# Two changes to a two-layer decoder step: the small attention products of the first layer in two parts, and the second layer's gates without an absolute value

## The chip, the cores and the metric

The kernel runs on one core of one Trainium2 chip. The metric is the device time of one launch in microseconds (us), the median of three runs. The engines are named as in the profile: PE (TensorE, with PEld for its weight loads), DVE (VectorE), ACT (ScalarE), POOL (GpSimd) and SP, from whose queue all transfers of data start.

## What is computed

A step of a two-layer decoder with D = 1024 over 512 prompt tokens and 8 sequences of 8 sample tokens (576 tokens together). The first layer is a gated linear recurrence with 16 heads of 128. The second is sliding-window attention with 32 query heads over shared keys and values, whose output is multiplied by silu of a gate. Everything is in float32. The parts that the change touches:

```python
# first layer, per head and chunk of the recurrence
att = einsum('bhtsd,bhsd->bhts', qc[:, :, :, None, :] * exp(rel), kc)   # masked, causal
o = o + einsum('bhts,bhse->bhte', att, vc)
# second layer
q, gate = split(rms_norm(x, g_norm) @ w_in, 2, axis=-1)
return x + (o * silu(gate)) @ w_out
```

## The kernel before

**Products.** Float32 accuracy comes from splitting both operands of a large product into a high and a low part and adding three products: a 128 x 1024 block of weights arrives in a buffer raw, ACT casts it to whi (L200), and DVE (first layer) or POOL (second layer) subtracts to get wlo (L204). One projection of one head in the first layer is three terms of 16 matmuls of 288 columns (L228): xhi with whi, xlo with whi, xhi with wlo. The second layer makes the same in halves of the tokens (L211).

**First layer.** A head has four projections, in the order pf (forget gate, tile pf), pq (query), pi (value), pg (output gate), and a recurrence, head_rec. The two are two generators: woven runs the recurrence of head h while it advances the projections of head h + 1. At each `yield ASK[i]` the recurrence asks that so many twelfths of the projections be issued first: ASK begins 3, 4, 5, so one term of a product lies between two neighbouring yields. Every fourth head also has blocks of the output product (tile po) in that list, and the last head has those alone.

**The small products.** The chunk attention of a head is four chunks (NC) of 128 tokens, and each chunk is 20 small float32 products (L795) of 8 to 32 rows and 8 to 64 columns, placed in a 32-row part of the array by tile_position, all written to one PSUM tile pa. The trace counts 2,560 matmuls and 2,560 weight loads of L795 for the 16 heads, 160 of each per head. Two products smg (L806) for the sample tokens follow. Then DVE copies pa under a mask to att (L814) and smg to atts (L817). In the meantime DVE and ACT work on the forget gate of the next head: on DVE ka (L592) and lf (L595) read pf, ACT computes on them (L593, L596, L597), and DVE ends with L599. Later come pkt and pks (transposes), the states S (pu on PE, S on ACT at L848 and DVE at L850), and poT (L869, L887), which needs att and the states.

**Second layer.** Eight units (four groups of two); unit i has queries (q), gates (g) and an attention, and ORDER lists in which order the large products of q, g and o are issued while the attention steps run. An attention step makes the scores sc, DVE scales and reduces them (L1101, L1121), ACT takes exponentials (L1126), DVE and POOL scale (L1135), PE transposes (ptr, ptm), ACT and DVE split them (ph, pl at L1156, pk at L1163), PE makes pav, DVE joins it (ao, L1187) and multiplies by the gate (L1191, in place in sgt). A gate piece (m = 0 to 15, two per unit) is two half products pbg. ACT copies each to sgt (L1311), DVE copies the sample columns to sgS (L1313), and silu turns sgt into the gated factor: Abs, Exp, Ln on ACT (L1338 to L1340), min and subtract on DVE (L1341), Exp on ACT (L1342), and a multiply (L1343) on POOL, or on DVE for sgS.

**What sets the order.** A scheduler places each instruction on its engine's queue by priority; early(...) and high_priority move instructions forward. Each engine then runs its queue in order, and an instruction that waits for another engine holds all behind it.

The lines of silu before, where x is sgt or sgS and l a scratch tile:

```python
def silu(x, l, eng=dve):
    act.activation(l, x, AF.Abs)
    act.activation(l, l, AF.Exp, scale=-1.0)
    act.activation(l, l, AF.Ln, bias=1.0)
    dve.scalar_tensor_tensor(l, x, 0.0, l, ALU.min, ALU.subtract)
    act.activation(l, l, AF.Exp)
    eng.tensor_tensor(x, x, l, ALU.mult)
```

Of the kernel before, what the change touches and what calls it, by code (L numbers as in the profile page):

```python
# [15 lines left out]
AF = mybir.ActivationFunctionType  # L16
ALU = mybir.AluOpType
# [10 lines left out]
HN = T // 2  # L28
DI = 2048
NH = 16  # L30
NC = LP // P
# [6 lines left out]
SPAN = 40.0  # L38
# [13 lines left out]
ASK = (3, 4, 5, 6, 7, 8, 9, 10)  # L52
# [31 lines left out]
def yoco_kernel(  # L84
# [26 lines left out]
    act, dve, pool, pe, sp = nc.scalar, nc.vector, nc.gpsimd, nc.tensor, nc.sync  # L111
# [20 lines left out]
    def half(name):  # L132
        return ps["m"].tile([P, 512], F32, tag="m", name=name)

    def early(by=EARLY):
        return tc.high_priority(offset=by)
# [389 lines left out]
    with ExitStack() as actx:  # L526
# [153 lines left out]
        def head_rec(h, st, outs):  # L680
# [106 lines left out]
            part[16] = 0, 16, 16, 16  # L787
            turns = "64:0 64:1 32:2 0:3 0:2 24:3 0:1 32:0 8:3 24:2 16:3 0:0 8:2 24:1 16:2 8:1 24:0 16:1 8:0 16:0"
            for c in range(NC):
                for x in turns.split():  # L790
                    level, j = [int(v) for v in x.split(":")]
                    keys, queries = Ks[8 if level == 24 else level]
                    s0, ns, t0, nt = part[level]
                    s0, t0 = 32 * j + s0, (64 if level == 64 else 32 * j + t0)
                    pe.matmul(  # L795
                        pa[32 * j : 32 * j + ns, c, t0 : t0 + nt],
                        keys[:, c * P + s0 : c * P + s0 + ns],
                        queries[:, c * P + t0 : c * P + t0 + nt],
                        start=True,
                        stop=True,  # L800
                        tile_position=(0, 32 * j),
                    )
# [9 lines left out]
                    tile_position=(0, 32 * j),  # L812
                )
            dve.copy_predicated(att, view(m_ge, [[0, NC], [1, P]]), pa)  # L814
            yield ASK[1]
            ats = att_s[i2]
            dve.copy_predicated(  # L817
                view(ats[:LS, :], [[32, 4], [1, 16]]),
# [55 lines left out]
            for bb in [2 * j + i for i in range(2) for j in range(4)]:  # L874
                j = bb // 2
# [80 lines left out]
        for h in range(NH):  # L956
            nxt, chunks, n = {}, [], 0
# [21 lines left out]
    with ExitStack() as bctx:  # L979
# [34 lines left out]
        with tc.tile_pool(name="kvx", bufs=1) as kvx:  # L1014
# [4 lines left out]
            for c0 in range(0, 4, 2):  # L1019
                ws = [split_weights(kvw[c], f"kv{c}") for c in (c0, c0 + 1)]  # L1020
                kf = [kvx.tile([P, T], F32, tag=f"kf{c % 2}", name=f"kf{c}", bufs=2) for c in (c0, c0 + 1)]
                for j in range(2):
                    for c in range(2):
                        pm = half(f"pkv{c0 + c}_{j}")
# [274 lines left out]
        def gates(i, sgS, sgt):  # L1299

            g, pp = i // 2, i % 2
            for pr in range(2):
                m = 2 * i + pr
                c = DI + m * P
                w = split_weights(w_in_b[0, :, c : c + P].rearrange("(k p) c -> p k c", p=P), f"bg{m}")
                for j in range(2):
                    pm = half(f"pbg{m}_{j}")
                    product_half(pm, *w, bx, j)
                    n = min(HN, LP - j * HN)
                    with early(EARLYB):  # L1310
                        act.copy(sgt[:, pr, j * HN : j * HN + n], pm[:, :n])  # L1311
                        if j == 1:
                            dve.tensor_copy(sgS[:, 2 * pp + pr, :], pm[:, n:HN])  # L1313
                    if j == 1:
                        silu(sgt[:, pr, :], ab.tile([P, LP], F32, tag="lb", name=f"lb{m}", bufs=1), pool if SILU_POOL else dve)
                        if pp == 1 and pr == 1:
                            silu(sgS, ab.tile([P, 4, LS], F32, tag="oS", name=f"lbs{g}", bufs=1))
                    yield
# [16 lines left out]
                    yield  # L1335

        def silu(x, l, eng=dve):
            act.activation(l, x, AF.Abs)  # L1338
            act.activation(l, l, AF.Exp, scale=-1.0)
            act.activation(l, l, AF.Ln, bias=1.0)  # L1340
            dve.scalar_tensor_tensor(l, x, 0.0, l, ALU.min, ALU.subtract)  # L1341
            act.activation(l, l, AF.Exp)  # L1342
            eng.tensor_tensor(x, x, l, ALU.mult)  # L1343

        def new_group(g):
# [227 lines left out]
```

## Time and profile before

| what | value |
|---|---|
| median of three runs | 1188.15 us (1186.46 to 1188.95) |
| profiled execution | 1186.25 us, of which the span from first to last instruction is 1184.5 us |
| PE busy | 1115.6 us, 94% of the span, 10,937 matmuls |
| DVE busy | 901.2 us, 76% |
| ACT busy | 725.7 us, 61% |
| POOL busy | 340.2 us, 29% |
| mean granted PE clock | 0.977 of full speed |

Busy is the time in which an engine has an instruction in work. The idle time of PE is what is left of its span, 69 us. In a view of waits a line gives the engine that waits, the line waited for, and the sum; "issue" is time for which the profile shows no releaser. The first layer runs from about 30 us to 700 us in the profiled execution, the second from about 735 us to the end. The rows that are read are in the section ahead of the prediction.

### The profile page before, as it was taken

The page shows a single profiled execution, that of the slowest core. Times are in us where ns is not written, and L with a number is a line of the kernel's source. Part 1 is how long each engine was busy: PE and PEld are TensorE (multiplying, and loading weights), DVE is VectorE, ACT ScalarE, POOL GpSimd, SP SyncE. Part 2 cuts the span into 40 slices and gives each one's busy share as a digit, 9 for nine tenths or more (in the row PEclk, how much of TensorE's full clock was granted, in tenths as well). Part 3 has the DMA queues.
Part 4 walks back from the last instruction along what each step waited for, and adds up shares of the span by engine and source line. Part 5 has one row for each costly group of instructions (what it writes and reads, how often), then busy time and mean ns, then how long its engine had stood idle before and what let it go on. Part 6 is the DMA issues. An engine that isn't in the chain of part 4 may idle for free.

```text
span 1184.5 us, 27353 instructions
## 1 busy us (share of the span) xinstructions
PE 1115.6 (94%) x10937; PEld 1082.3 (91%) x10937; DVE 901.2 (76%) x2078; ACT 725.7 (61%) x1752; POOL 340.2 (29%) x311
## 2 busy tenths in 40 slices
PE   5999999998999989999999987989999989999997
PEld 4999999998998989999989877989989989998986
DVE  8897776589883597784887779567887788676686
ACT  6776763466772566762766455667746765776545
POOL 1122221121111132120212155544544453444440
PEclk8999999999999999999999998989999999999998
DMA  5332233232432423332332322211211212112102
GB/s 152 99 110 85 82 111 108 65 100 78 121 128 65 127 67 107 110 92 75 92 108 73 103 72 72 68 54 55 72 54 55 87 47 83 55 55 71 55 19 81
DMA packets 161097, 98.01 MB, mean 83 GB/s; under 512 B 3897, under 2 KB 157546, under 8 KB 160938
## 3 DMA queue, kind: packets, MB, share of 16 engines
q1 hardware_dynamic: 160970, 96.26, 27.7%
q8 instruction: 86, 1.41, 0.5%
q14 instruction: 41, 0.34, 0.1%
HBM read 84.06 MB, written 14.16 MB: 83 GB/s over the span
## 4 chain that ended last, share of the span: by engine, by line
PE 40%; DVE 13%; ACT 8%; issue 3%; POOL 1%; DVEq 0%; ACTq 0%; POOLq 0%
PE pbg L211 6%; PE po L211 5%; PE pbq L211 5%; PE po L228 4%; PE pg L228 3%; PE pf L228 3%; PE pi L228 2%; ACT P L1126 2%; PE pkv L211 2%; PE sc L1097 2%; PE pq L228 1%; DVE P L1101 1%; PE pav L1180 1%; PE pz L211 1%; DVE QS L1288 1%
## 5 line engine op out<-in xcount | busy, mean ns | idle before, releaser
L606 POOL TENSOR_TENSOR Xl<-Xl 128x72 f32<-128x72 f32 x80 | 50.1, 656 | 212.3 <-DVE Xl L603 211.1
L638 POOL TENSOR_TENSOR sg<-sg,lg 128x576 f32<-128x576 f32 x16 | 26.3, 1642 | 277.8 <-ACT lg L571 277.8
L200 ACT CAST whi_a<-raw_a 128x1024 fp32r<-128x1024 f32 x64 | 67.1, 1049 | 62.1 <-PE po L228 31.6
L204 DVE TENSOR_TENSOR wlo_a<-raw_a,whi_a 128x1024 fp32r<-128x1024 f32 x64 | 81.7, 1282 | 26.2 <-issue 24.2
L1126 ACT ACTIVATE P<-P,st 128x192 f32<-128x192 f32 (+2 forms) x128 | 54.2, 425 | 65.4 <-DVE st L1121 65.3
L1135 POOL TENSOR_SCALAR P<-P,st 128x192 f32<-128x192 f32 (+1 forms) x64 | 48.9, 774 | 110.6 <-DVE st L1128 87.1
L438 DVE TENSOR_TENSOR hT<-hT,po 128x576 f32<-128x576 f32 x32 | 24.1, 754 | 47.2 <-PE po L228 46.9
L200 ACT CAST whi_o<-raw_o 128x1024 fp32r<-128x1024 f32 x30 | 31.4, 1047 | 29.8 <-PE po L228 25.3
L204 POOL TENSOR_TENSOR wlo_bg<-raw_bg,whi_bg 128x1024 fp32r<-128x1024 f32 x16 | 38.3, 2396 | 32.7 <-ACT whi_bg L200 31.1
L228 PE MATMUL po<-oh,whi_o 128*128 128x288 f32 x256 | 43.4, 305 | 4.4 <-ACT whi_o L200 1.9
L211 PE MATMUL po<-ohb,whi_o 128*128 128x288 f32 x224 | 43.7, 311 | 2.3 <-DVE hT L1333 1.4
L211 PE MATMUL po<-olb,whi_o 128*128 128x288 f32 x224 | 42.2, 301 | 3.9 <-DVE olb L1395 2.0
L662 POOL TENSOR_TENSOR vb<-vst,bmask 128x512 fp32r<-128x512 f32 x32 | 36.7, 1167 | 26.7 <-DVE vst L658 13.8
L204 POOL TENSOR_TENSOR wlo_bq<-raw_bq,whi_bq 128x1024 fp32r<-128x1024 f32 x16 | 38.6, 2417 | 19.6 <-ACT whi_bq L200 19.5
L228 PEld LDWEIGHTS po<-oh,whi_o 128*128 128x128 f32 x256 | 36.9, 192 | 6.3 <-ACT whi_o L200 2.2
L228 PE MATMUL pq<-xhi,whi_a 128*128 128x288 f32 x256 | 38.4, 298 | 3.7 <-issue 3.7
L211 PE MATMUL pbq<-xhi,whi_bq 128*128 128x256 f32 (+1 forms) x256 | 41.7, 307 | 0.0
L211 PE MATMUL pbg<-xhi,whi_bg 128*128 128x288 f32 x256 | 41.3, 304 | 0.3 <-ACT QS L1285 0.3
L211 PE MATMUL pbq<-xlo,whi_bq 128*128 128x256 f32 (+1 forms) x256 | 41.1, 305 | 0.0
L228 PE MATMUL po<-ol,whi_o 128*128 128x288 f32 x256 | 41.0, 297 | 0.0
L211 PE MATMUL pbg<-xlo,whi_bg 128*128 128x288 f32 x256 | 40.9, 304 | 0.0
L211 PE MATMUL pbg<-xhi,wlo_bg 128*128 128x288 f32 x256 | 40.8, 303 | 0.0
(389 smaller groups left out, 3792.0 us busy)
## 6 DMA issues: line engine op xcount, KB each, us to landing
raw_a<-in_w_in_a_dram SPq DMA_DIRECT2D x64, 512.0 KB
S<-in_state_hgrn_dram SPq DMA_DIRECT2D x32, 256.0 KB
out_dram<-S SPq DMA_DIRECT2D x32, 256.0 KB
raw_o<-in_w_out_a_dram SPq DMA_DIRECT2D x16, 512.0 KB
raw_bq<-in_w_in_b_dram SPq DMA_DIRECT2D x16, 512.0 KB
raw_bg<-in_w_in_b_dram SPq DMA_DIRECT2D x16, 512.0 KB
raw_o<-in_w_out_b_dram SPq DMA_DIRECT2D x16, 512.0 KB
xt<-in_x_prompt_dram SPq DMA_DIRECT2D x4, 512.0 KB
```

The source lines that it names most:

```text
L200: act.copy(hi[:, :n], raw[:, :n])
L204: eng.tensor_tensor(lo[:, r], raw[:, r], hi[:, r].bitcast(F32), ALU.subtract)
L211: pe.matmul(pm[:, : c1 - c0], w[:, k * width + w0 : k * width + w0 + P], x(k)[i][:, c0:c1], start=n == 0, stop=n == len(terms) - 1,)
L228: pe.matmul(pm[:, j, :HN], w[:, k * width + c0 : k * width + c0 + P], x(k, j), start=n == 0 and k == 0, stop=n == 2 and k == nk - 1,)
L438: dve.tensor_add(h2, h2, ps2(pm))
L606: pool.tensor_tensor(X8[:, :, j : j + 1], X8[:, :, j : j + 1], X8[:, :, k : k + 1], ALU.add)
L638: (pool if SGP else dve).tensor_tensor(sg, sg, l, ALU.mult)
L662: pool.tensor_tensor(t, view(vst.bitcast(F32), [[0, 4], [1, P]], off=half * P), view(bmask, [[1, 4], [0, P]]), ALU.mult,)
L1097: pe.matmul(sc[:, hf, k0[hf] :], QS[pr][:, 2 * n + hf, :], kk[:, g, ks], start=q == 0, stop=q == 1)
L1101: dve.tensor_tensor_reduce(Pt[:, pr, hf, k0[hf] :], sc[:, hf, k0[hf] :], amask[:, k0[hf] :], 0.125, NEG, ALU.add, ALU.max, accum_out=st[:, ...
L1126: act.activation(x, x, AF.Exp, bias=st[:, a : a + 1], accum_out=st[:, 8 + a : 9 + a])
L1135: (pool if e == "p" else dve).tensor_scalar(x, x, st[:, 8 + a : 9 + a], None, ALU.mult)
```

## The change

The loop over the four chunks yields once in its middle, and the yield that stood between the two masked copies is gone. So the recurrence asks for the next step of the projections after two chunks instead of after four and smg. In the second layer DVE takes the halves of pbg out of PSUM, clamped from below at -40 (SPAN), and silu is x times exp(-ln(1 + exp(-x))): three activations instead of four, without the step on DVE. This is the form of the first layer's silu_arg.

```diff
--- before.py
+++ after.py
@@ -787,6 +787,8 @@
             part[16] = 0, 16, 16, 16
             turns = "64:0 64:1 32:2 0:3 0:2 24:3 0:1 32:0 8:3 24:2 16:3 0:0 8:2 24:1 16:2 8:1 24:0 16:1 8:0 16:0"
             for c in range(NC):
+                if c == NC // 2:
+                    yield ASK[1]
                 for x in turns.split():
                     level, j = [int(v) for v in x.split(":")]
                     keys, queries = Ks[8 if level == 24 else level]
@@ -812,7 +814,6 @@
                     tile_position=(0, 32 * j),
                 )
             dve.copy_predicated(att, view(m_ge, [[0, NC], [1, P]]), pa)
-            yield ASK[1]
             ats = att_s[i2]
             dve.copy_predicated(
                 view(ats[:LS, :], [[32, 4], [1, 16]]),
@@ -1308,9 +1309,9 @@
                     product_half(pm, *w, bx, j)
                     n = min(HN, LP - j * HN)
                     with early(EARLYB):
-                        act.copy(sgt[:, pr, j * HN : j * HN + n], pm[:, :n])
+                        dve.tensor_scalar(sgt[:, pr, j * HN : j * HN + n], pm[:, :n], -SPAN, None, ALU.max)
                         if j == 1:
-                            dve.tensor_copy(sgS[:, 2 * pp + pr, :], pm[:, n:HN])
+                            dve.tensor_scalar(sgS[:, 2 * pp + pr, :], pm[:, n:HN], -SPAN, None, ALU.max)
                     if j == 1:
                         silu(sgt[:, pr, :], ab.tile([P, LP], F32, tag="lb", name=f"lb{m}", bufs=1), pool if SILU_POOL else dve)
                         if pp == 1 and pr == 1:
@@ -1335,11 +1336,10 @@
                     yield
 
         def silu(x, l, eng=dve):
-            act.activation(l, x, AF.Abs)
+
+            act.activation(l, x, AF.Exp, scale=-1.0)
+            act.activation(l, l, AF.Ln, bias=1.0)
             act.activation(l, l, AF.Exp, scale=-1.0)
-            act.activation(l, l, AF.Ln, bias=1.0)
-            dve.scalar_tensor_tensor(l, x, 0.0, l, ALU.min, ALU.subtract)
-            act.activation(l, l, AF.Exp)
             eng.tensor_tensor(x, x, l, ALU.mult)
 
         def new_group(g):
```

Where the instructions stand before and after the change, in three places. The first is PE in the recurrence of head 0, which runs under the projections of head 1 (G and KL are the operands of the small products, pq is head 1's query product). Before:

```order
L795 MATMUL pa<-G_0_668 16x16
L795 MATMUL pa<-G_0_672 8x8
L795 MATMUL pa<-G_0_668 16x16
L806 MATMUL smg_847<-KL_676 32x64 x2
L228 MATMUL pq_857<-xhi,whi_a_0_853 128x288 x16
L228 MATMUL pq_857<-xlo,whi_a_0_853 128x288 x16
L827 MATMUL pkt_891<-ident,KQ_374 128x128 x4
```

After:

```order
L797 MATMUL pa<-G_0_672 8x8
L797 MATMUL pa<-G_0_668 16x16
L228 MATMUL pq_813<-xhi,whi_a_0_809 128x288 x16
L797 MATMUL pa<-G_0_659 32x64 x2
L797 MATMUL pa<-G_0_665 32x32
...
L797 MATMUL pa<-G_0_672 8x8
L797 MATMUL pa<-G_0_668 16x16
L808 MATMUL smg_870<-KL_676 32x64 x2
L228 MATMUL pq_813<-xlo,whi_a_0_809 128x288 x16
L828 MATMUL pkt_891<-ident,KQ_374 128x128 x4
```

One term of pq (16 matmuls of 288 columns) moved from behind smg to the middle of the small products. In the heads with output blocks it is two blocks of po (24 matmuls each), in the last head one of 12.

The second place is DVE beside it: the forget gate of head 1 (ka, lf) and the masked copies of head 0. Before:

```order
L592 SCALAR_TENSOR_TENSOR ka_751<-pf_698,lf_747 128x576
L814 COPY_PREDICATED att<-m_ge,pa 128x512
L595 SCALAR_TENSOR_TENSOR lf_747<-pf_698,lf_747 128x576
L817 COPY_PREDICATED atts_358<-m_310,smg_847 64x4x16
L599 SCALAR_TENSOR_TENSOR lf_757<-ka_751,ln1m,lf_747 128x576
```

After:

```order
L592 SCALAR_TENSOR_TENSOR ka_751<-pf_698,lf_747 128x576
L595 SCALAR_TENSOR_TENSOR lf_747<-pf_698,lf_747 128x576
L816 COPY_PREDICATED att<-m_ge,pa 128x512
L599 SCALAR_TENSOR_TENSOR lf_757<-ka_751,ln1m,lf_747 128x576
L818 COPY_PREDICATED atts_358<-m_310,smg_870 64x4x16
```

Both copies moved one place back, each behind an instruction of the forget gate.

The third is DVE in the second layer, attention of unit 0 with the second gate piece (pbg_1 is its second half). Before:

```order
L1135 TENSOR_SCALAR P_0_2_9982<-P_0_2_9982,st_0_2_9983 128x192 x2
L1313 COPY sgS_9709<-pbg_1_10030 128x64
L1187 TENSOR_TENSOR ao_0_0_10083<-pav_0_0_10077,low_0_0_10081 64x256 x2
L1156 TENSOR_TENSOR pl_0_1_10096<-ptr_0_1_10087,ph_0_1_10095 128x512
L1341 SCALAR_TENSOR_TENSOR lb_10057<-sgt_9860,lb_10057 128x512
L1163 TENSOR_TENSOR pk_0_1_10099<-ptm_0_1_10088,pk_0_1_10099 64x256
L1288 TENSOR_TENSOR QS_0_10104<-pbq_0_10112,QS_0_10104 64x4x64 x2
L1163 TENSOR_TENSOR pk_0_1_10099<-ptm_0_1_10088,pk_0_1_10099 64x256
L1191 TENSOR_TENSOR sgt_9860<-ao_0_0_10083,sgt_9860 128x2x128
```

After:

```order
L1129 RECIPROCAL st_0_2_9981<-st_0_2_9981 128x4
L1312 TENSOR_SCALAR sgt_9860<-pbg_1_10028 128x224
L1314 TENSOR_SCALAR sgS_9709<-pbg_1_10028 128x64
L1136 TENSOR_SCALAR P_0_2_9980<-P_0_2_9980,st_0_2_9981 128x192 x2
L1188 TENSOR_TENSOR ao_0_0_10079<-pav_0_0_10073,low_0_0_10077 64x256 x2
L1157 TENSOR_TENSOR pl_0_1_10092<-ptr_0_1_10083,ph_0_1_10091 128x512
L1192 TENSOR_TENSOR sgt_9860<-ao_0_0_10079,sgt_9860 128x2x128
L1164 TENSOR_TENSOR pk_0_1_10095<-ptm_0_1_10084,pk_0_1_10095 64x256 x2
L1289 TENSOR_TENSOR QS_0_10100<-pbq_0_10108,QS_0_10100 64x4x64 x2
```

The gate's eviction to sgt is new on DVE, ahead of the scaling of P; the step lb of silu is gone; and the multiply by the gate (sgt from ao) moved from behind pk to ahead of it. PE's and POOL's order in the second layer is as it was.

## Rows read from the trace of the kernel before

**Rows 1.** The page, part 1 (busy us, share of the span, instructions) and part 3 (instruction queue q8: packets, MB, share of the 16 DMA engines).
```profile
PE 1115.6 (94%) x10937; PEld 1082.3 (91%) x10937; DVE 901.2 (76%) x2078; ACT 725.7 (61%) x1752; POOL 340.2 (29%) x311
q8 instruction: 86, 1.41, 0.5%
```

**Rows 2.** The waits of PE over the whole run: us in total, times, longest us.
```profile
PE pq L228 <- issue: 3.7, 3, 2.6
PE pa L795 <- issue: 2.8, 3, 2.0
PE poT L887 <- DVE S L850: 4.3, 11, 0.9
```

**Rows 3.** Windows from the start of the span to the end of five gaps of PE in the small products: width, then PE busy and (x matmuls), PEld busy and (x weight loads), DVE, ACT, POOL, granted clock, DMA share, GB/s.
```profile
0.00:62.83 62.83, 49.25 (x473) 47.01 (x474) 53.72 (x124) 41.70 (x84) 14.43 (x23) 0.92 0.44 127
0.00:95.08 95.08, 80.89 (x853) 77.80 (x854) 79.44 (x173) 64.83 (x136) 21.63 (x31) 0.95 0.41 118
0.00:294.78 294.78, 274.96 (x3136) 267.09 (x3137) 235.35 (x476) 188.23 (x405) 55.92 (x73) 0.98 0.34 99
0.00:501.59 501.59, 474.61 (x5418) 460.70 (x5419) 387.97 (x757) 312.28 (x675) 91.56 (x113) 0.98 0.34 101
0.00:596.07 596.07, 566.29 (x6433) 550.69 (x6434) 454.17 (x874) 364.49 (x786) 106.29 (x129) 0.99 0.34 99
```

**Rows 4.** Timeline of PE in the visit to the small products of head 7: start us, us, instruction, count.
```profile
324.67 2.29 PE L228 MATMUL pf<-xhi,wlo_a 128*128 128x288 f32 x16
326.89 0.25 PE L795 MATMUL pa<-G 128*32 128x64 f32 x3
328.19 0.21 PE L795 MATMUL pa<-KL 128*32 128x32 f32 x1
328.86 2.35 PE L228 MATMUL pq<-xhi,whi_a 128*128 128x288 f32 x16
331.04 2.24 PE L228 MATMUL pq<-xlo,whi_a 128*128 128x288 f32 x16
333.12 0.60 PE L827 MATMUL pkt<-ident,KQ 128*128 128x128 f32 x4
```

**Rows 5.** Timeline of PE, the two longest gaps (in brackets the idle time before the row and its releaser).
```profile
294.79 0.20 PE L795 MATMUL pa<-G 128*8 128x8 f32 x2 [1.98 <-issue]
596.08 1.20 PE L228 MATMUL pq<-xhi,whi_a 128*128 128x288 f32 x8 [2.61 <-issue]
```

**Rows 6.** Timelines of DVE, ACT and PE in two heads in which DVE is late (head 9, and for the last row head 5).
```profile
431.28 0.73 DVE L814 COPY_PREDICATED att<-m_ge,pa 128x512 f32<-128x512 uint8 x1
431.39 0.78 ACT L593 ACTIVATE KQ<-ka,ln1m 128x576 f32<-128x576 f32 x1 [2.57 <-DVE ka L592]
431.90 0.74 DVE L595 SCALAR_TENSOR_TENSOR lf<-pf,lf 128x576 f32<-128x576 f32 x1
432.73 0.78 ACT L596 ACTIVATE ka<-lf,lndf 128x576 f32<-128x576 f32 x1 [0.56 <-DVE lf L595]
442.44 0.49 PE L887 MATMUL poT<-S,KQ 128*128 128x128 f32 x2 [0.88 <-DVE S L850]
443.30 0.49 PE L887 MATMUL poT<-S,KQ 128*128 128x128 f32 x2 [0.37 <-DVE S L850]
264.23 1.16 PE L842 MATMUL pu<-vt,kt 128*128 128x128 f32 x8 [1.25 <-ACT kt L829]
```

**Rows 7.** A window of 5 us behind the first of these heads, columns as in rows 3 after the stretch.
```profile
445.00:450.00 5.00, 5.00 (x30) 4.87 (x30) 4.19 (x10) 3.45 (x13) 0.00 (x0) 0.75 0.13 39
```

**Rows 8.** Lines of the gates, and of the eviction of the first layer's gate: engine, operation, out<-in, count, duration in ns (least/median/most), first and last start, shapes.
```profile
L1311 ACT COPY sgt<-pbg x32: 328/359/402, 753.4 to 1099.1; 128x288 f32<-128x288 f32 x16, 128x224 f32<-128x224 f32 x16
L1338 ACT ACTIVATE lb<-sgt x16: 629/632/638, 758.9 to 1099.5; 128x512 f32<-128x512 f32 x16
L1341 DVE SCALAR_TENSOR_TENSOR lb<-sgt,lb x16: 677/693/1600, 761.0 to 1101.9; 128x512 f32<-128x512 f32 x16
L1341 DVE SCALAR_TENSOR_TENSOR lbs<-sgS,lbs x4: 412/415/420, 810.7 to 1102.5; 128x256 f32<-128x256 f32 x4
L1313 DVE COPY sgS<-pbg x16: 210/225/226, 758.7 to 1099.5; 128x64 f32<-128x64 f32 x16
L563 DVE TENSOR_SCALAR sg<-pg x16: 745/750/757, 55.2 to 654.5; 128x576 f32<-128x576 f32 x16
```

**Rows 9.** The waits of DVE in the gates over the whole run: us in total, times, longest us.
```profile
DVE lb L1341 <- ACT lb L1340: 7.9, 9, 1.7
DVE sgS L1313 <- ACT sgt L1311: 4.2, 9, 1.6
```

**Rows 10.** Timelines of POOL, DVE and PE in the second layer's first unit.
```profile
772.33 1.30 POOL L1343 TENSOR_TENSOR sgt<-sgt,lb 128x512 f32<-128x512 f32 x1 [1.63 <-ACT lb L1342]
773.67 0.42 DVE L1191 TENSOR_TENSOR sgt<-ao,sgt 128x256 f32<-128x256 f32 x1 [0.84 <-POOL sgt L1343]
786.12 0.70 PE L1204 MATMUL scs<-kcT,Qs 128*64 128x128 f32 x4 [3.05 <-DVE Qs L1293]
```

**Rows 11.** Timelines of DVE and PE, and a window of 5 us, around 954 us, where two gate pieces have just ended.
```profile
953.32 0.68 DVE L1341 SCALAR_TENSOR_TENSOR lb<-sgt,lb 128x512 f32<-128x512 f32 x1
954.50 0.38 PE L1180 MATMUL pav<-pk,Vd 128*128 128x256 f32 x1 [1.22 <-DVE pk L1163]
955.00:960.00 5.00, 5.00 (x25) 4.98 (x24) 3.72 (x14) 3.50 (x14) 3.45 (x5) 0.66 0.01 3
```

## The prediction

> **What bounds the kernel now.** I read the page first: PE is busy for 94% of the span [rows 1], DVE for 76%, so time is won only where PE stands still or is slowed, 69 us in all. Then the waits of PE. In the first layer the largest have no releaser: 2.8 us inside the small products and 3.7 us at the query product right behind them, together 6.5 us in six gaps, of which the two longest are 1.98 and 2.61 us [rows 2, 5]. Next come the waits of poT for the states that DVE makes, 4.3 us. In the second layer PE waits for single late DVE instructions, the longest 3.05 us [rows 10].
>
> What are the gaps without releaser? PE and PEld instructions that had started by the end of five of them, added up: 947, 1707, 6273, 10837, 12867 [rows 3]. The differences are 760, 4566, 4564, 2030. Divided by 3, 18, 18 and 8 they all give 253.3 to 253.8. The whole stream is 21,874 such instructions and came in 86 instruction packets, 254 each [rows 1]. So every gap lies on the border between two packets of instructions: PE has used one up and the next isn't there. It happens only here because the small products run at about 11 ns for a matmul with its load (below), so a packet of 254 lasts some 1.4 us, and in an ordinary term (2.08 us for 16) over 16 us.
>
> **Part one, the gaps.** In the new order 32 instructions of a term of pq, 2.08 us long, stand between the halves. A packet that lies across them lasts at least 222 small instructions (1.2 us), 2.08 us and the change of mode, 3.7 us in all; one that ends inside the term lasts longer. The two longest gaps say how long the next packet took, counted from the start of the packet before it: about 1.4 + 2.0 = 3.4 us, and 1.4 + 2.6 = 4.0 us or, with the products between, somewhat more. So the first goes and a rest below 1 us stays of the last. I take 6.0 of the 6.5 us as gained (bounds 6.5 and 0).
>
> [...]
>
> **Part one, a second visit.** Small products use the array in another shape than the large ones, and going there and back costs PE time that the profile books as busy. In head 7 the third term of pf starts at 324.67 and the second of pq at 331.04: 6.37 us. An undisturbed term lasts 333.12 - 331.04 = 2.08 us, two of them 4.16, so the visit took 2.21 us [rows 4]. Inside it three chunks lie between 326.89 and 328.19, 0.43 us each, so four chunks and smg are 1.77 us of work, and 0.44 us is the change of shape, there and back. The new order makes two visits per head. No row shows a second visit that has nothing to wait for, so it is bounded: 0.44 us if all of it is the change of shape, 0 if it is all waiting of the first product for its operands. The first is nearer, since the visit follows without an idle row. I take 0.4 us: 16 x 0.4 = +6.4 us (bounds 0 and 7.0). So the two effects nearly cancel on PE itself.
>
> **Part one, DVE.** The masked copy att (0.73 us) leaves its place between ka and lf. In the late head 9 lf would start 0.62 us earlier, and ACT's L596 with it, but not before L593 ends at 432.17, so 0.56 us earlier instead of 432.73 [rows 6]. All that follows on DVE up to the states moves with it, and att falls into the time in which DVE waits for ACT anyway. att and smg end later by a term, which nobody notices: poT comes three terms later. What is late next is poT, where PE now arrives 0.4 us later and the states 0.56 us earlier: up to 1.0 us of wait per head can go. In the two late heads there is that much (0.88 + 0.37 us at poT, and 1.25 us at pu for kt, which ACT copies behind L596) [rows 6]: -2.0 us. The other heads share 4.3 - 2 x 1.25 = 1.8 us of poT's wait [rows 2]; of that I take -1.1. [...] Part one: +6.4 - 6.0 - 2.0 - 1.1 - 0.8 = -3.5 us.
>
> **Part two, the second layer's gates.** ACT loses 32 copies of 0.359 us, and one activation in each silu, 16 of 0.632 and 4 of about 0.4 us: 23 us [rows 8]. DVE loses 16 steps lb of 0.693 us (one was stretched to 1.6) and 4 of 0.415: 12.7 us. It gains 32 evictions, which the trace does not show. The line between the 64-column copy (0.225) and the 576-column eviction of the first layer (0.750) is 1.03 ns a column: 0.456 us for 288 and 0.39 for 224 columns, 13.5 us for 16 of each. The 64-column instruction stays. So DVE's work stays the same within 1 us, but two of its waits go, 7.9 us for ACT in the middle of silu and 4.2 us for ACT's copy [rows 9]. DVE now waits for PE where ACT did; queued behind it are the next softmax and splitting steps.
>
> None of this is on PE, and PE's order here is the same. It gains only where a gate step stands right before the DVE instruction that PE waits for. That is seen at 954.50: PE waited 1.22 us for pk, and lb, 0.68 us, ran just before it; behind the wait a slice has a clock of 0.66, 1.7 us lost [rows 11]. The longest wait, 786.12, follows softmax steps without a gate step and stays. I take 0.7 us, half of that slice's 1.7, and 0.5 us elsewhere: -2.0 us (bounds: -6, half of the 12.1 us of DVE waits, and +10, the slower rival).
>
> **Sum.** Profiled execution 1186.25 - 3.5 - 2.0 = 1180.75 us. It lies 1.9 us under the median of the runs shown, so against the median: 1188.15 - 5.5 = **1182.65 us**, 1182.6.
>
> **Rivals.**
> 1. The second visit is nearly free and the clock keeps full speed in the slices named: another -6.4, 1176.2. For it: PE shows no idle row there. Against: the 0.44 us is counted from starts of terms, idle or not.
> 2. The gaps stay: the next packet is late whatever PE does in between, so that each gap moves to the next border. That takes back 6.0 us: 1188.6, no change. For it: the gap of 2.61 us sits behind the first matmul of pq, not in the small products [rows 5]. Against: no gap lies on a border away from them. [...]
> 3. The change does on PE what it says but the waits are not taken up, and the gates don't matter: 1182.65 + 2 + 2 = 1186.6, no change that can be told.
> 4. Slower: the multiply by the gate, L1191, now stands ahead of pk and holds it while POOL finishes sgt. Before, DVE waited there 0.84 us with pk already done [rows 10]. If in each of the eight units POOL's 1.30 us multiply is waited for on PE's path, that is 8 x 1.3 = +10.4 in place of -2.0: 1195.0. It decides from (3.5 + 2.4) / 8 = 0.74 us a unit. Against: ACT hands sgt to POOL earlier by one activation and a round trip to DVE, and PE's next instructions often do not need pk for some us.
>
> **How the numbers follow.** Two runs of this kernel can be told apart at about 0.2%, 2.4 us. Chances: forecast 0.42 (own range 1178 to 1185.7), rival 1 0.15, rival 2 0.13, rival 3 0.16, rival 4 0.14. Faster is the forecast, rival 1 and a part of rival 3: 0.60. Slower is rival 4: 0.14. The rest, 0.26, is no change. The range 1175 to 1191 takes in rivals 1 to 3 and leaves out most of rival 4 and the lower end of rival 1.
>
> **What would show it.** The waits of PE without releaser at the small products and the query product fall from 6.5 to under 1 us; if they stay, rival 2. From the start of pf's third term to pq's third, less three terms of 2.08 us, is 2.6 us per head where one visit took 2.21; if 2.2, rival 1. The waits of poT for S fall from 4.3 to about 1.5 us. DVE's new evictions take 0.46 and 0.39 us; PE's waits for pk and pl (L1163, L1156) show whether rival 4 holds. I am wrong most easily in the second layer, where single waits of 1 to 3 us and the slower clock behind them depend on which instruction of DVE comes first.

## The result, and the profile after

The changed kernel takes **1170.84 us** (median of 4 runs, 1169.39 to 1171.89) against 1188.51 for the kernel before (4 runs on the same chip, 1186.46 to 1188.95): a ratio of 0.9861, interval 0.9838 to 0.9884, 17.7 us faster. The forecast was 1182.6 in a range of 1175 to 1191: the right sign, and less than a third of the gain. The profiled execution took 1169.39 us, its span 1167.6.

Where did 16.9 us of span go? Two views of windows, PE alone; columns: stretch, its length, PE busy (matmuls), granted clock, DMA share, GB/s. The first row of each runs from the first matmul of pf to the second term of pq in the last head, the second from the first matmul of pbq to the last of po. The kernel before:

```profile
23.86:631.37 607.51, 590.67 (x6813) 0.99 0.33 96
733.83:1156.29 422.46, 403.91 (x3106) 0.97 0.20 58
```

The kernel after:

```profile
23.19:625.72 602.53, 592.11 (x6813) 0.99 0.33 97
726.40:1139.44 413.04, 398.74 (x3106) 0.98 0.20 59
```

The same matmuls run in both. The first layer is 5.0 us shorter, the second 9.4. The rest, 0.7 us at the start and 1.8 between the layers, is not the change: that middle took 100.6 to 102.5 us in all the profiles below but one (e6, 104.8), and the changed kernel alone has had both (100.67 here, 102.25 in e16, the same kernel again). Most of that difference is one wait, of PE at pkv for DVE's xlo (L467): 1.5 us in the profile before, none in the one after.

In the first layer PE stands still 6.4 us less (607.51 - 590.67 = 16.8, now 10.4) and is busy 1.4 us longer. In the second it stands 4.2 us less (18.5, now 14.3) and is busy 5.2 us less with the same work; some 3.7 of that is the clock (the granted clock is 0.5 of full speed for 24.3 us of that stretch before and for 16.8 after, summed over the clock's slices; half of that time is counted as lost).

Waits of PE after, us in total, times, longest us; they answer to [rows 2].

```profile
PE poT L888 <- DVE S L851: 3.5, 7, 0.7
PE poT L888 <- ACT S L849: 1.2, 2, 0.7
PE pa L797 <- issue: 1.1, 1, 1.1
PE pu L843 <- ACT kt L830: 0.8, 2, 0.5
PE sc L1098 <- DVE QS L1289: 0.7, 1, 0.7
PE pav L1181 <- DVE pl L1157: 0.5, 1, 0.5
```

The waits without releaser have gone from 6.5 us to 1.1, those of poT have hardly moved, and pk is no longer in the list. In the timeline of PE, head 7 [rows 4] now reads:

```profile
324.14 2.29 PE L228 MATMUL pf<-xhi,wlo_a 128*128 128x288 f32 x16
326.36 0.25 PE L797 MATMUL pa<-G 128*32 128x64 f32 x3
327.34 2.38 PE L228 MATMUL pq<-xhi,whi_a 128*128 128x288 f32 x16
329.64 0.25 PE L797 MATMUL pa<-G 128*32 128x64 f32 x3
330.74 2.38 PE L228 MATMUL pq<-xlo,whi_a 128*128 128x288 f32 x16
```

From 324.14 to 330.74 are 6.60 us; less two terms of 2.08 that leaves 2.44 for both visits, where one took 2.21. The second visit costs **0.23 us**, not 0.4. The whole first layer agrees: PE's busy time there, less what the clock cost, is 585.2 to 586.1 us in the eleven profiles below with one visit (e7 left out, which adds products) and 587.9 to 589.2 in the six with two, some 3.1 us for 16 heads. (The forecast named pq's third term for this count; pkt stands ahead of that one, so it goes to the second here, as the forecast's own 6.37 us do.)

The new gate steps, grouped by line and shape (busy us, mean ns | idle before):

```profile
L1312 DVE TENSOR_SCALAR sgt<-pbg 128x288 f32<-128x288 f32 x16 | 7.3, 453 | 3.8 <-PE pbg L211 3.7
L1312 DVE TENSOR_SCALAR sgt<-pbg 128x224 f32<-128x224 f32 x16 | 6.1, 381 | 1.1 <-PE pbg L211 1.0
```

0.453 and 0.381 us, as estimated (0.456 and 0.39). DVE's busy time went from 901.2 to 895.4, ACT's from 725.7 to 702.1. So the sizes of the gate steps were right, and what the new gates are worth to PE was not.

### The profile page after: what moved, and what is told of

Read it like the earlier page. It is cut to its first block, busy times and chain, and to the rows that moved or that the text cites. A ratio compares the mean times of both kernels' runs of the same rounds, so it can differ in the third digit from the quotient of the medians.

```text
span 1167.6 us, 27339 instructions
## 1 busy us (share of the span) xinstructions
PE 1111.7 (95%) x10937; PEld 1078.1 (92%) x10937; DVE 895.4 (77%) x2090; ACT 702.1 (60%) x1700; POOL 340.7 (29%) x311
## 4 chain that ended last, share of the span: by engine, by line
PE 45%; DVE 11%; ACT 6%; issue 2%; POOL 1%; DVEq 0%; ACTq 0%; POOLq 0%
PE pbg L211 7%; PE po L211 7%; PE pbq L211 5%; PE po L228 4%; PE pg L228 3%; PE pf L228 3%; PE pi L228 3%; PE pq L228 2%; PE pkv L211 2%; PE sc L1098 2%; ACT P L1127 1%; PE pav L1181 1%; PE pz L211 1%; DVE QS L1289 1%; PE pa L797 1%
## 5 line engine op out<-in xcount | busy, mean ns | idle before, releaser
L204 DVE TENSOR_TENSOR wlo_a<-raw_a,whi_a 128x1024 fp32r<-128x1024 f32 x64 | 81.8, 1282 | 25.0 <-issue 23.6
L204 POOL TENSOR_TENSOR wlo_bg<-raw_bg,whi_bg 128x1024 fp32r<-128x1024 f32 x16 | 38.4, 2402 | 35.5 <-ACT whi_bg L200 30.0
L204 POOL TENSOR_TENSOR wlo_bq<-raw_bq,whi_bq 128x1024 fp32r<-128x1024 f32 x16 | 38.8, 2430 | 19.2 <-ACT whi_bq L200 19.1
L211 PE MATMUL po<-ohb,wlo_o 128*128 128x288 f32 x224 | 41.3, 301 | 0.0
L228 PE MATMUL po<-oh,wlo_o 128*128 128x288 f32 x256 | 40.4, 294 | 0.0
L204 POOL TENSOR_TENSOR wlo_o<-raw_o,whi_o 128x1024 fp32r<-128x1024 f32 x14 | 33.6, 2399 | 22.0 <-ACT whi_o L200 20.3
```

Source lines behind the costliest of these rows:

```text
L204: eng.tensor_tensor(lo[:, r], raw[:, r], hi[:, r].bitcast(F32), ALU.subtract)
L211: pe.matmul(pm[:, : c1 - c0], w[:, k * width + w0 : k * width + w0 + P], x(k)[i][:, c0:c1], start=n == 0, stop=n == len(terms) - 1,)
L228: pe.matmul(pm[:, j, :HN], w[:, k * width + c0 : k * width + c0 + P], x(k, j), start=n == 0 and k == 0, stop=n == 2 and k == nk - 1,)
```

## The experiments

Ratios are of runs to the kernel before on the same chip, with 95% intervals. Of the profile of each kernel three columns tell about the second layer, in us: "second layer" is the length of the stretch above, "PE still" is that length less PE's busy time, and "clock" is half of the time at the lower clock, an estimate of what it cost, as above. Before has 422.5, 18.5 and 12.1, after 413.0, 14.3 and 8.4. What is left, the work itself, is 389 to 393 us in all nineteen profiles. So the larger differences between two kernels are of standing still or of the clock.

### Do the two parts add up?

e1_visits has the first two pieces of the diff, e2_gates the last two. e3_evict takes of e2 only the evictions, e4_silu only the new silu:

```diff
# e3_evict
-act.copy(sgt[...], pm[:, :n])
+dve.tensor_scalar(sgt[...], pm[:, :n], -SPAN, None, ALU.max)
-    dve.tensor_copy(sgS[...], pm[:, n:HN])
+    dve.tensor_scalar(sgS[...], pm[:, n:HN], -SPAN, None, ALU.max)
# e4_silu
-act.activation(l, x, AF.Abs)
-act.activation(l, l, AF.Exp, scale=-1.0)
+act.activation(l, x, AF.Exp, scale=-1.0)
 act.activation(l, l, AF.Ln, bias=1.0)
-dve.scalar_tensor_tensor(l, x, 0.0, l, ALU.min, ALU.subtract)
-act.activation(l, l, AF.Exp)
+act.activation(l, l, AF.Exp, scale=-1.0)
```

> Part one alone (the small products in two visits, masked copy behind the second; gates as before). Theory A, which the trace of after suggests: the parts add up, and the second layer's gain belongs to the gates. Then this kernel is 6.0 us faster than before (1182.5), all of it gained before the first block of the second layer, and the second layer takes as long as before within 1 us. By the forecast's terms it is 3.5 us faster (1185.0). Rival B: the second layer's gain comes with any shift of its start against the transfers and packets, whatever the gates do. Then the second layer changes here by 4 us or more although nothing in it is edited, and the kernel is 10 us or more faster. In all theories: gaps of PE without releaser 6.5 -> 1 to 2 us, pf's third term to pq's second less two terms 2.44 us against 2.22.

> Part two alone (gates on DVE and three activations; small products as before). Theory A: 9.5 us faster than before (1179.0), all of it in the second layer, with two or three fewer slices of 5 us at a granted clock below 0.7 there, and the first layer as before within 1 us. The forecast's term: 2.0 us faster (1186.5). Rival B (any shift of the second layer's start): 2 us faster or less, since its start has not moved.

> Half of part two: DVE takes the gates' halves under a maximum, silu keeps Abs and the step lb on DVE. ACT loses 11.5 us of copies, DVE gains 13.5 us and both waits of the chain for the other engine stay except that for ACT's copy. If the second layer's gain is the relief of ACT's queue from copies: 5 us faster or more. If it is that DVE no longer has a step in the middle of silu (with the pk behind it): no change within 2 us, and PE's wait of about 1.2 us for pk in unit 5 stays.

> The other half of part two: silu as the new one (Exp, Ln, Exp on ACT, multiply on POOL), ACT copies the halves as before. It leaves out the lower limit of -40 on the gate. DVE loses 12.7 us of steps lb and stands no more in the middle of silu, ACT loses 11.7 us. If the step lb ahead of PE's operands is what held PE: 6 us faster or more. If ACT's copies were it: 2 us faster or less.

| run | median us | ratio | second layer | PE still | clock |
|---|---|---|---|---|---|
| e1_visits | 1180.08 | 0.9949 (0.9928 to 0.9969) | 421.3 | 18.2 | 11.7 |
| e2_gates | 1175.93 | 0.9918 (0.9894 to 0.9943) | 412.8 | 14.4 | 8.2 |
| e3_evict | 1188.50 | 1.0015 (1.0000 to 1.0030) | 427.4 | 21.1 | 14.0 |
| e4_silu | 1173.89 | 0.9895 (0.9872 to 0.9917) | 411.4 | 12.2 | 8.6 |

The parts add up: 0.51% and 0.82% are 6.1 and 9.7 us, 15.8 together, where the whole change has 17.7 above and 14.7 in e16. e1 leaves the second layer within 1.2 us of before, and e2 shortens it as the whole change does: rival B, a gain by the shifted start alone, falls. Within part two the new silu does everything; DVE's eviction alone makes the second layer 4.9 us longer, and beside the new silu 1.4 (412.8 against 411.4). In both cases PE stands still longer by it, by 2.6 and 2.2 us; in the ratios of e2 and e4 it can't be told. A wait of ACT in the changed kernel (us in total, times, longest us):

```profile
ACT lb L1340 <- DVE sgt L1312: 5.7, 8, 1.1
```

### What in silu was it?

All four start from e4_silu (so without the lower limit) and put one thing back or move one.

```diff
# e8_hop2: a DVE step with two inputs in the middle again (behind Ln)
+dve.scalar_tensor_tensor(l, x, 0.0, l, ALU.mult, ALU.add)
# e9_hop1: the same with one input
+dve.tensor_scalar(l, l, 0.0, None, ALU.max)
# e10_act: one more pass of ACT ahead
+act.copy(l, x)
+act.activation(l, l, AF.Exp, scale=-1.0)
-act.activation(l, x, AF.Exp, scale=-1.0)
# e12_muldve: the last multiply on DVE
-SILU_POOL = True
+SILU_POOL = False
```

> The silu of the run with the new silu alone, and in its middle again a DVE step on lb of the same form as the old one (x times 0 plus lb: two inputs from SBUF, value unchanged). So against before only one activation of each silu is gone. It leaves out the lower limit of -40 on the gate. Theory C: what held PE is the DVE step, which stands ahead of PE's operands and, reading two inputs from SBUF, is itself held while POOL runs. Then at most 3 us of the 11 to 12.5 us stay gained. Theory D: what held PE is ACT's time per silu: 8 us or more stay gained.

> As the run before, but the DVE step reads one input (lb's maximum with 0, value unchanged). It leaves out the lower limit of -40 on the gate. If the step costs by being held while POOL runs: no lb step over 1 us, and 8 us or more of the gain come back. If it costs by the handover from ACT to DVE and back and by its own time: the same time as with two inputs, within 2 us.

> The new silu with one more pass on ACT ahead of it (a copy of x to lb), and no DVE step; ACT has four activations per silu again. It leaves out the lower limit of -40 on the gate. Theory C (DVE step): within 2.5 us of the run with the new silu alone, 10 us or more under before. Theory D (ACT's time): at most 4 us under before.

> The new silu with ACT's copies, and its last multiply on DVE instead of POOL (it leaves out the lower limit of -40 on the gate). DVE gets 16 steps of some 0.7 us back, at the end of silu and not in its middle, so no activation of ACT's queue waits for DVE; POOL has 16 steps of 1.3 us fewer. If the old step lb cost by standing in the middle (ACT's queue waits behind it): the time of the run with the new silu alone, within 2.5 us, 10 us or more under before. If it cost as work on DVE ahead of PE's operands: 5 us or more over that run.

| run | median us | ratio | second layer | PE still | clock | ACT's wait for DVE's lb |
|---|---|---|---|---|---|---|
| e8_hop2 | 1185.38 | 0.9997 (0.9980 to 1.0013) | 421.1 | 21.0 | 7.0 | 14.3 |
| e9_hop1 | 1179.84 | 0.9935 (0.9910 to 0.9959) | 415.9 | 15.0 | 10.6 | 11.1 |
| e10_act | 1177.85 | 0.9935 (0.9911 to 0.9960) | 418.0 | 14.5 | 13.7 | none |
| e12_muldve | 1175.02 | 0.9912 (0.9889 to 0.9935) | 410.1 | 12.1 | 7.2 | none |

Taking away Abs alone (e8 against before) gains nothing in time, but that does not make Abs free. With one activation less ahead of it, the DVE step now fell into POOL's subtraction of weights (L204): it took over 0.85 us in 14 of 16 pieces, where before has three such, and ACT waited 14.3 us behind it, where before waited 5.8. Taking away the DVE step alone (e10 against before) gains 0.65%, both together 1.05%. So neither theory holds alone: e10 is 0.4% or 4.7 us over e4, where C allowed 2.5, and 7.7 under before, where D allowed 4. The first of these is weak in the time, since the intervals overlap; PE stands still 2.3 us longer in e10 than in e4, and the rest is the clock (13.7 against 8.6). e12 decides on DVE: 16 steps of DVE are back, at the end of silu, and PE stands still no longer than in e4. It was not work on DVE as such that cost, though POOL has 16 steps fewer in exchange, which may hide a part. e9 missed its purpose: the step with one input was held by POOL all the same (14 of 16 took over 0.6 us, all while L204 ran on POOL), and ACT waited behind it. The lines of the step in e8 and in e9 (duration min/median/max in ns); before has 677/693/1600 [rows 8].

```profile
L1341 DVE SCALAR_TENSOR_TENSOR lb<-sgt,lb x16: 679/1246/2360, 760.9 to 1101.0; 128x512 f32<-128x512 f32 x16
L1341 DVE TENSOR_SCALAR lb<-lb x16: 414/971/2099, 761.0 to 1095.3; 128x512 f32<-128x512 f32 x16
```

What e8, e9 and e10 share is that silu occupies ACT's queue for longer, by a pass or by a wait. Whether that reaches PE through ACT's queue or through a late sgt, two more runs on e4_silu tell apart:

```diff
# e13_late: sgt later, ACT not held
+if eng is pool:
+    pool.tensor_copy(l, l)
 eng.tensor_tensor(x, x, l, ALU.mult)
# e14_behind: ACT held, sgt not later
+if eng is pool:
+    act.copy(spare, l)
 eng.tensor_tensor(x, x, l, ALU.mult)
```

> The new silu with ACT's copies (limit of -40 left out), and POOL copies lb onto itself ahead of its multiply: sgt comes later by one POOL step, ACT is not held. If the lateness of sgt is the way to PE: 4 us or more over the run with the new silu alone (a ratio to before of 0.993 or more). If ACT's queue is the way: within 2.5 us of that run (0.9875 to 0.9915).

> The new silu with ACT's copies (limit of -40 left out), and behind its last activation one more pass of ACT that nobody reads: ACT's queue is held by one pass more per gate piece, sgt is not later. If what stands behind silu on ACT's queue is the way to PE: 4 us or more over the run with the new silu alone (0.993 or more, as with the pass ahead of silu). If the lateness of sgt is the way: within 2.5 us of that run.

| run | median us | ratio | second layer | PE still | clock |
|---|---|---|---|---|---|
| e13_late | 1171.17 | 0.9878 (0.9853 to 0.9904) | 406.4 | 11.6 | 3.4 |
| e14_behind | 1177.20 | 0.9935 (0.9913 to 0.9958) | 414.7 | 14.5 | 9.7 |

A later sgt costs nothing: in e13 it is ready 2.12 us after ACT's last activation instead of 1.39 (medians), and PE stands still no longer than in e4. A pass that nobody reads, behind silu, costs PE 2.3 us of standing still, as the one ahead of it does. So the cost comes **with what is queued on ACT**, and not through sgt. Whether the queue itself does it is not shown: the scheduler also put 13 of DVE's 2,058 instructions in another order in e14, and 12 to 15 in e8 to e10 (3 in e13), and the second place below is one where that counts.

### How ACT's queue reaches PE

In the first of two places the step from ACT to PE is DVE's, and POOL decides how long that takes. Timeline of the kernel before (DVE, POOL and PE), just ahead of [rows 11]:

```profile
949.44 2.39 POOL L204 TENSOR_TENSOR wlo_bq<-raw_bq,whi_bq 128x1024 fp32r<-128x1024 f32 x1
949.49 2.62 DVE L1191 TENSOR_TENSOR sgt<-ao,sgt 128x256 f32<-128x256 f32 x1
952.90 0.38 PE L1180 MATMUL pav<-pl,Vc 128*128 128x256 f32 x1 [1.28 <-DVE pl L1156]
```

The same place after:

```profile
937.81 0.43 DVE L1192 TENSOR_TENSOR sgt<-ao,sgt 128x256 f32<-128x256 f32 x1
937.88 2.62 POOL L204 TENSOR_TENSOR wlo_bq<-raw_bq,whi_bq 128x1024 fp32r<-128x1024 f32 x1 [0.24 <-ACT whi_bq L200]
941.96 0.30 PE L1181 MATMUL pav<-ph,Vc 128*128 128x256 f32 x1
942.63 0.36 PE L1181 MATMUL pav<-pk,Vd 128*128 128x256 f32 x1
```

L1191 took 0.43 us after, but 2.62 before, where POOL's subtraction (2.39) had begun 0.05 us ahead of it. Behind it on DVE stand pl and pk, and PE waited 1.28 and 1.22 us and then had a granted clock of 0.66 from 955 to 960 us [rows 11]; after, DVE is 0.07 us ahead and PE has no idle row there. In both orders the instruction that began first kept its usual length and the other ran longer: L204 took 2.39 us and L1191 2.62 before, L1191 0.43 and L204 2.62 after. This step, the 15th of 32 on its line, took 2.4 to 2.6 us in five of the six profiles with the old silu (all but e5, below) and 0.43 in all 13 with a shorter one. So the hold goes with the long silu, though 0.05 us can spare one. It is one place and not the whole: e8 is free of it and PE stands still for 21.0 us there. Summed over all DVE steps of the second layer that ran over 0.25 us past the shortest of their line and shape, before has 50 us of holding and after 40, but e4, where PE stands still for less time than after, has 45. So it is not the sum of the holds that PE pays, but where they fall.

A second place, in e14_behind (DVE, ACT and PE):

```profile
1027.44 0.42 DVE L1255 TENSOR_TENSOR oS<-oS,sgS 128x256 f32<-128x256 f32 x1
1027.95 0.39 ACT L1265 CAST ohb<-oS 128x64 fp32r<-128x64 f32 x2 [1.86 <-DVE oS L1255]
1029.47 2.44 DVE L1266 TENSOR_TENSOR olb<-oS,ohb 128x64 fp32r<-128x64 f32 x1 [0.87 <-ACT ohb L1265]
1038.27 0.27 PE L1097 MATMUL sc<-KDh,QS 128*128 128x64 f32 x1 [2.14 <-DVE QS L1288]
```

and in e4_silu (DVE and PE):

```profile
1021.61 0.41 DVE L1255 TENSOR_TENSOR oS<-oS,sgS 128x256 f32<-128x256 f32 x1
1024.68 2.70 DVE L1266 TENSOR_TENSOR olb<-oS,ohb 128x64 fp32r<-128x64 f32 x3
1033.74 0.27 PE L1097 MATMUL sc<-KDh,QS 128*128 128x64 f32 x1 [0.73 <-DVE QS L1288]
```

PE's wait for QS is 2.14 us, as the kernel before has it (2.12), against 0.73. One of the three small olb is long in both (2.44 us, and 2.43 of the 2.70 in e4, where POOL's L204 began 0.01 us before them and took 2.49), so that is not the difference. It is that DVE waits for ACT's ohb in e14, 0.37 and 0.87 us, and ACT for DVE's oS, 1.86 us: there oS stands behind pk and the steps of the next softmax on DVE's queue, where e4 has it right behind pl. Before and e10 have oS at a late place too, and waits of 2.12 and 2.0 (e12 and e15 as well, but without such a wait). So 1.4 of the 2.3 us of e14 come where the order on DVE has changed with the pass, and no run here parts the one from the other.

### The first layer's terms

```diff
# e5_att, against before: one visit, the masked copy behind the term
-dve.copy_predicated(att, view(m_ge, [[0, NC], [1, P]]), pa)
 yield ASK[1]
+dve.copy_predicated(att, view(m_ge, [[0, NC], [1, P]]), pa)
# e6_three, against e1: three visits
-if c == NC // 2:
-    yield ASK[1]
+if c in (1, 3):
+    yield ASK[1 if c == 1 else 2]
# e7_shift, against before: 160 more instructions at the start
+for _ in range(3):
     pe.transpose(px[:, k, :], ...)
```

> One visit of the small products as before, only DVE's masked copy att stands behind the term that follows (behind lf of the next head instead of ahead of it); gates as before. By the forecast's terms for DVE's order: 3.9 us faster (2.0 + 1.1 + 0.8), poT's waits for S 4.3 -> 1.5 us. By the trace of the changed kernel, where poT's waits stayed and only pu's for kt fell: 1 us faster, within 0.2% of before. The gaps of PE without releaser stay at 6 to 7 us in both.

> The small products in three visits (one chunk, two chunks, one chunk with smg), a term of pq between each; gates as before. Price of a visit: by the trace of the changed kernel 0.22 us each, so that pf's third term to pq's third, less three terms, is 2.66 us in an undisturbed head, and this kernel is 16 x 0.22 = 3.5 us over the one with two visits, less the one gap of 1 us left there: ratio to before 0.997. By the forecast's 0.4 us per visit: 5.4 us over it, ratio to before 0.9995.

> The kernel before, with each transposition of the input at the very start made three times: 80 more matmuls and 80 more weight loads ahead of all else, nothing else changed. If the gaps lie on borders of packets of 254 instructions, all borders come 160 instructions earlier in the program: the gaps leave visits 1, 2, 7, 9, 12 and 14 of the small products (of 16), where they were, and come in some of visits 3, 4, 5, 8, 10, 11 and 16, where a packet of under 2.5 us now ends. If the gaps belong to these heads (a transfer or another engine that is late there), they stay in visits 1, 2, 7, 9, 12 and 14. The whole may be some us longer for the added work.

**e5_att**: 1184.81 us, 0.9995 (0.9975 to 1.0015). DVE's order alone gains nothing; the waits of poT for DVE's S were 3.9 us before, up to pq of the last head, and are 4.4 here.

**e6_three**: 1205.54 us, 1.0173 (1.0143 to 1.0203), some 26 us over two visits, which no theory had. The visit itself is not what costs: against e1, head 7 is 0.42 us earlier at pq's first term, with one chunk less ahead of it, and 0.65 later from there to pq's third, so 0.23 for one visit more. PE's waits for kt have risen from 0.8 us in two heads (e1) to 22.8 us in 12. Timelines of ACT and PE:

```profile
349.17 0.68 ACT L735 ACTIVATE KL<-Xl 128x576 f32<-128x576 f32 x1 [2.63 <-POOL Xl L606]
349.75 0.57 ACT L830 COPY kt<-pkt 128x512 f32<-128x512 f32 x1
350.37 0.82 PE L843 MATMUL pu<-vt,kt 128*128 128x128 f32 x5 [1.34 <-ACT kt L830]
```

With the third visit the copy kt stands behind an activation of the next head, which waits 2.63 us for POOL. pkt, its operand, had been done by 346.7.

**e7_shift**: a single run, 1191.21 us. The gaps moved where the border count puts them. PE, and a window from the start to the end of the first of them, with PE's and PEld's counts:

```profile
134.34 0.24 PE L796 MATMUL pa<-G 128*16 128x16 f32 x4 [1.95 <-issue]
339.36 0.84 PE L228 MATMUL pq<-xhi,whi_a 128*128 128x288 f32 x5 [0.66 <-issue]
437.51 0.24 PE L807 MATMUL smg<-KL 128*32 128x64 f32 x1 [1.85 <-issue]
666.46 0.69 PE L228 MATMUL po<-ol,whi_o 128*128 128x288 f32 x4 [1.51 <-issue]
```

```profile
0.00:134.33 134.33, 123.31 (x1362) 118.25 (x1362) 107.87 (x226) 89.71 (x190) 28.01 (x39) 0.97 0.38 110
```

They lie in visits 3, 8, 10 and 16, all among the seven foretold, and visits 1, 2, 7, 9, 12 and 14 have none. 1362 + 1362 = 2,724 instructions had started; less the 947 of the first border before [rows 3] that is 7.0 packets of 253.6. The one gap that the changed kernel keeps, at 591.65 (1.10 us), comes after 6,432 + 6,433 = 12,865: 47.0 packets. So the gaps are packets that come late.

### Versions that combine

e11_both is e1 with the new silu and ACT's copies, e15_best the same with the multiply on DVE, e17_more e11 with POOL's copy of e13 (these three without the lower limit), e16_after the changed kernel again.

> The small products in two visits and the new silu, while ACT keeps the copies of the gates' halves (it leaves out the lower limit of -40 on the gate). If the parts add up: 6.1 + 12.5 = 18.6 us under before, a ratio of 0.984, some 1 to 2 us under the changed kernel. If DVE's eviction helps once the small products are split: 3 us or more over the changed kernel.

> Two visits, the new silu with ACT's copies and its multiply on DVE (limit of -40 left out). If the parts add up: 6.1 + 10.5 to 13 us under before, a ratio of 0.984 to 0.986, the same as the changed kernel or up to 2 us under it.

> The changed kernel once more, beside the runs of this call: 0.986 of before.

> Two visits, the new silu with ACT's copies (limit of -40 left out), and POOL's copy of lb onto itself ahead of its multiply. If the parts add up: 0.9878 and 0.9949 of before make 0.983, some 3 to 5 us under the changed kernel (0.9861 and 0.9876). If the shorter second layer in that run was chance of one execution: as the changed kernel within 2 us.

| run | median us | ratio | second layer | PE still | clock |
|---|---|---|---|---|---|
| e11_both | 1169.93 | 0.9862 (0.9838 to 0.9886) | 410.3 | 12.5 | 7.2 |
| e15_best | 1168.82 | 0.9855 (0.9828 to 0.9882) | 411.6 | 10.9 | 11.6 |
| e16_after | 1171.37 | 0.9876 (0.9849 to 0.9903) | 414.0 | 14.6 | 8.9 |
| e17_more | 1163.71 | 0.9827 (0.9803 to 0.9852) | 407.4 | 11.8 | 4.7 |

e11 and e15 can't be told from the changed kernel. e17 has the lowest time of all, 1163.71, 7 us under both medians of the changed kernel, though its interval still overlaps theirs. What POOL's copy adds to e11 is the clock: PE stands still about as long, and the mean granted clock of the runs is 0.986 against 0.981.

## Why the prediction was wrong

**Part one** was forecast at -3.5 us and measured -6.1. Term by term:

- Gaps -6.0: right, by the reason given. 6.5 us fell to 1.1, and e7 shows the packets. What was off is the rest of the last gap, forecast below 1 us: the packet came 1.10 us late even with a term in between. Rival 2 falls.
- Second visit "I take 0.4 us: 16 x 0.4 = +6.4": **too dear by half**. It was 0.23 in head 7, 16 x 0.23 = 3.7 (3.1 by the busy time of the whole layer). The step at fault took all that is not chunks, 0.44 us, for change of shape. The other half, 0.21 us, was paid once per head in any case. Between the forecast and rival 1.
- Late heads -2.0 and other heads -1.1: **wrong**. poT's waits for DVE stayed at 3.5 us where 1.5 was forecast, and e5 shows that the masked copy's place is worth nothing. Only pu's wait for kt fell, 1.7 to 0.8.
- Clock -0.8: no run shows this term. The slice behind head 9 had a granted clock of 0.75 before [rows 7]; after, the clock reads 1.00 from 435 to 450 us, though PE still waited 0.66 and 0.37 us for S in that head. The clock's loss in the whole first layer went from 5.3 to 3.3 us in the two profiles, but it varies from run to run by more than that (5.3 to 9.7 in eleven profiles with one visit, 3.2 to 7.9 in six with two), so what the change brought of it is not decided.

From the two profiles: idle -6.4, clock -2.0, visits +3.7, sum -4.7 of the 5.0 us seen.

**Part two** was forecast at -2.0 us and measured -9.7, beyond even its bound of -6. The failed step is "It gains only where a gate step stands right before the DVE instruction that PE waits for." It looked for gate steps on DVE. The runs put the cost in silu's chain on ACT: four passes and a wait for DVE in their middle, with copies and casts behind them (ohb, ph, pk, QS) for which DVE and PE wait later. Without the fourth pass and the DVE step PE stands still 6.3 us less (e4, 12.2 against 18.5); one pass put back costs 2.3, the DVE step 2.8 (e9) to 8.8 (e8), and a step on DVE at the chain's end nothing that shows (e12). At 954.50 the row named lb as what ran before pk; the row 3.8 us earlier, L1191 at 2.62 us instead of 0.43, was busy time and so in no list of waits. The bound, half of DVE's waits, was taken from the wrong engine. In the two profiles the 9.4 us are 4.2 of standing still, 3.7 of the clock and 1.4 of busy time that no run explains; the forecast had counted 0.85 for the clock, in one slice.

The eviction on DVE, which the forecast let stand as neutral, costs 1.4 us of second layer beside the new silu (4.9 beside the old). ACT now waits 5.7 us for DVE there; that this is what PE pays is likely, but no run shows it.

Rival 4 (L1191 held while POOL finishes sgt, slower) did not come about: DVE waits for POOL's sgt once, 1.8 us, and e13 shows that a later sgt costs nothing. But that POOL holds DVE at L1191 was the right place to look: held by its other work, and in the kernel before.

What stays open: how the 4.2 us of standing still divide among the places in the second layer, how much of them is ACT's queue and how much the scheduler's other order on DVE, and what makes the clock fall less often in one kernel than in another (3.4 us lost in e13, 13.7 in e10).

## What to carry to other kernels

Price a hand-over in the middle of a chain by asking who waits for the next instructions on that queue, and not by the waits at the step itself: here the one in silu went with 2.8 us (e9) to 8.8 us (e8) more of PE's standing still. Before a small difference is explained, take PE's standing still and the clock apart: half or more of the 0.4% between e10 and e4 was the clock. And an edit on one queue can make the scheduler order another one anew, so the order of all queues is part of what an experiment changes. A step that ran at several times its usual duration (L1191, 2.62 us instead of 0.43) was a wait which no list of waits showed; lay the other engine's timeline beside such a step before the cause is given to its neighbour. An extra visit cost PE 0.23 us here, but check what it moves on the other queues: with the third visit the run was some 26 us longer, and PE's waits for one copy, which ended up behind a late activation, rose from 0.8 to 22.8 us.

## What was not expected of the hardware

- Small DVE steps too ran until POOL's subtraction had ended: three 128x64 olb took 2.70 us together beside a subtraction of 2.49 (e4), where two of them took 0.37 in e14. A step with one input (e9) took up to 2.10 us instead of 0.41.
- At L1191 a lead of 0.05 to 0.07 us went with which engine took longer: DVE by 2.2 us (2.62 against 0.43) where POOL led, POOL by 0.2 (2.62 against 2.39) where DVE led.
- With a copy on POOL that changes no value the second layer was 5.0 us shorter in the profile (e13 against e4), and all of it is the clock (3.4 us lost against 8.6; PE stands still for 11.6 and 12.2). The ratios, 0.9878 and 0.9895, overlap, but e17 points the same way (0.9827 against 0.9862 for e11).
